# A decoder block by split float32 products: the rotary exchange moved to ScalarE, and five more steps by seven products

## The chip, the cores and the metric

The kernel runs on one core of one Trainium2 chip, in one launch. The metric is the device time of the launch in microseconds (us), the median of several runs. TensorE is called PE, VectorE DVE, ScalarE ACT and SyncE SP, as the profile does.

## The reference

One layer of a decoder block for 256 positions of width 2048, all in float32. Shortened to what is computed:

```python
a = rmsnorm(h, norm_mix_pre)
q_a, k_a, v_a, q_r, f_r, i_r, g_r, gate_a, gate_r = split_columns(a @ w_in)     # 2048 x 17408
qh, kh = rotary(heads(q_a), S), rotary(heads(k_a), S)    # rot = [-t[64:], t[:64]]; t * cos + rot * sin
attn = dilated_window_attention(...)      # 3 groups of 8 heads, mixed by their denominators
r_out = hgrn2_chunked(silu(q_r), log f, 1 - f, i_r)      # gated recurrence, normed, times silu(g_r)
y = sigmoid(gate_a) * (attn @ w_attn_branch) + sigmoid(gate_r) * (r_out @ w_hgrn_branch)
h = h + rmsnorm(y @ w_mix_out, norm_mix_post)
gt, up = split(rmsnorm(h, norm_ffn_pre) @ w_ffn_gate_up)     # 2048 x 11264
ff = (silu(gt) * up) @ w_ffn_down                        # 5632 x 2048
h = h + rmsnorm(ff, norm_ffn_post)
```

## The kernel before

Every weight matrix is streamed from HBM once. To keep float32 accuracy with the fast `fp32r` matmul, each weight and each activation is split into a high part (ACT copies it with rounding) and a low part (DVE subtracts: raw minus high), and each product is three matmuls: high x high, high x low, low x high. `mm` at L138 records nearly all of PE's matmuls, so most rows of PE carry that line.

The work is a list `items` that the loop at L1600 walks. An item is either a *chunk* (128 x 1024 weights, 16 matmuls in its common form; the stages of f, q, the rotary q and k, the branches) or a *step* of a *wide block* (two groups of 512 columns by 256 rows). The items' order is written out by hand, and so is what runs beside an item. In iteration `i`, `prepare(i)` splits item `i + 2` (AHEAD = 2), fetches sums for item `i + 4` and issues the load of raw weights as far as three raw buffers allow; then `multiply(i)` issues PE's work; then generators that wait in queues are advanced by one `yield` each: `evacs` (emptying PSUM), `lanes` (attention, recurrence, norms) and, in chunk items, `back` (weight sums). All engines run their instructions in that order, so an instruction that waits holds up what is behind it on its engine.

A wide step (m, 0) is plain: 2 x 2 x 2 products of 128 x 128 x 512, three matmuls each, 24 matmuls. A step "by seven" computes the same with seven products of sums of the operands, Strassen's way: 21 matmuls. It needs sums of the weights and sums of the activations (`seven_sums`, `pair_sums`, kept in `h7` for the FFN). In (m, 1) DVE forms the weights' sums (`sum`, L434, L440, L441), ACT and DVE split them into `hi` and `lo` (L439, L442, L447) and split three quarters of the raw weights into `dh` and `dl` (L445, L449). In (m, 2) the sums were formed long before, by `weight_sums`, and stored to DRAM as `presum`; `fetch_sums` brings them back as `s`, and only the splits are left (L426 to L430). `dh` and `dl` share four slots (tag "d"). Products go to eight PSUM banks, four called `acc` and four `aux`; in a block whose `flip` is false, the four plain sums take aux banks and the products p1, p5, p6 and p7 take acc banks. Within a step by seven PE first does the products of sums and then those of raw weights; in the last one of a block, and in the down blocks, the other way round.

After a block's last step by seven, `gather` (L506) joins p1, p5, p6 and p7; `evac_ffn` (L1376) adds them at the block's end; `turn_act` (L1339), after step 1 of the next block, transposes the finished block's output on PE into two PSUM banks (acc where `flip` is false), from which ACT copies it (L1349).

The FFN's gate and up weights are 11 blocks of 8 steps, numbered 0 to 10 by `j` at L1574; block 0 is plain, and GATE_UP3 and GATE_UP4 give the order of steps in the others. `w_ffn_down` follows as two blocks of 22 steps; there `prep_act` splits the activations and makes their sums for each step by seven.

`weight_sums` (L294) is one generator for all steps (m, 2). For each it loads 1 MB into the one buffer `pre`, lets four items pass, forms the sums with four DVE instructions in two items, and stores `presum` from ACT's queue; it moves by one `yield` per chunk item and is put off while `hold` is set in `recurrence`.

`evac_rope` (L873) applies the rotary step to a q or k block of two heads, transposed (head dimension in partitions): two DVE products of 64 partitions write the exchanged halves times sin to `w`, one more multiplies by cos, one adds.

Of the kernel before, what the change touches and what calls it, by code (L numbers as in the profile page):

```python
# [21 lines left out]
S = 256  # L22
# [19 lines left out]
    [(2, 0), (3, 0), (0, 1), (4, 0), (1, 1), (5, 0), (6, 0), (7, 0)],  # L42
]
GATE_UP3 = [(3, 0), (4, 0), (0, 2), (5, 0), (1, 1), (6, 0), (2, 2), (7, 0)]
GATE_UP4 = [(4, 0), (5, 0), (0, 2), (6, 0), (1, 1), (2, 2), (3, 1), (7, 0)]
PLACE = (0, 2, 1, 3)
DOWN = [[(m, m in by7) for m in range(KF // 2)] for by7 in (range(4, 20, 3), range(3, 19, 3))]

N_F, N_RAW, N_SPLIT, AHEAD, WARM, BRIDGE = 15, 3, 3, 2, 8, 6

# [50 lines left out]
def tile_hybrid_block(ctx: ExitStack, tc: tile.TileContext, t, out):  # L101
# [192 lines left out]
    def weight_sums(jobs):  # L294

        for n in jobs:
            x = fp[0].tile([P, 2048], F32, tag="pre", bufs=1, name=nm("pre"))
            b, i = steps[n][:2]
            m = b.order[i][0]
            for g in range(2):  # L300
                nc.sync.dma_start(
                    x[:, g * 1024 : (g + 1) * 1024].rearrange("p (k c) -> p k c", k=2),
                    b.w[2 * m * P : (2 * m + 2) * P, b.cols[g] : b.cols[g] + 512]
                    .rearrange("(k p) c -> p k c", p=P),
                )
            for _ in range(4):
                yield
            r = [x[:, q * 512 : (q + 1) * 512] for q in range(4)]
            nc.vector.tensor_sub(r[2], r[2], r[0])
            nc.vector.tensor_sub(r[0], r[1], r[0])  # L310
            yield
            nc.vector.tensor_add(r[1], r[1], r[2])
            nc.vector.tensor_sub(r[3], r[3], r[1])
            yield
            pre[n] = dram.tile([P, 2048], F32, name=nm("presum"))
            nc.scalar.dma_start(pre[n], x)
            yield
# [327 lines left out]
        return row[:, None, :].to_broadcast([P, n, S])  # L645

    evacs, turns, lanes, queue = deque(), deque(), [deque(), deque()], deque()
    back, hold = deque(), [False]
    ready = set()

    def advance(q):
# [43 lines left out]
    def opening():  # L695
        ss, s2 = small("ss"), small("s2")
        yield from sumsq(ss, xt)
        nc.sync.dma_start(gainr, t["hgrn_norm_gain"].to_broadcast([P, HW]))
        nc.sync.dma_start(cs, t["rope"])
        add_parts(s2[:, :2], ss)  # L700
        rsqrt_mean(r1c, s2[:, :2], D)
        ready.add("r1c")
        nc.scalar.preload_act_table_set("silu_and_others")
        yield from row_broadcast(rowb, r1c)
        ready.add("rowb")
        yield
        for _ in range(24):
            yield
        for i, (j, c) in enumerate(((0, -QSCALE), (1, -QSCALE), (0, 1.0), (1, 1.0))):
            nc.vector.scalar_tensor_tensor(  # L710
                out=tabs[:, i, :], in0=cs[:, j, :], scalar=c, in1=rowb, op0=OP.mult, op1=OP.mult
            )
            yield
        nc.sync.dma_start(amask, t["amask"])
        nc.sync.dma_start(lmask, t["lmask"])
# [157 lines left out]
    def evac_rope(key, tab, then=None):  # L873

        cos = tabs[:, tab, :]
        sin = tabs[:, tab + 1, :]

        def ev(i, src):
            if i == 0:
                qkT[key] = fslot("qk").rearrange("p (h t) -> p h t", h=4)  # L880
            yield
            w = ptile("w").rearrange("p (h t) -> p h t", h=2)
            for o, n in ((0, 64), (64, 0)):
                nc.vector.tensor_mul(
                    w[o : o + 64], src[n : n + 64],
                    sin[n : n + 64, None, :].to_broadcast([64, 2, S]),
                )
            yield
            u = src
            nc.vector.tensor_mul(u, src, by_rows(cos, 2))  # L890
            nc.vector.tensor_add(
                qkT[key][:, 2 * i : 2 * i + 2, :].rearrange("p h (two j) -> p h two j", two=2),
                u.rearrange("p h (j two) -> p h two j", two=2),
                w.rearrange("p h (j two) -> p h two j", two=2),
            )
            if i == 1 and then:
                then()
        return ev
# [339 lines left out]
    def mix_to_ffn(i):  # L1238
# [60 lines left out]
        ffn(2, 1)  # L1299
        residual_of(5, (0, 1), False)  # L1300

    def more_h(c):
        if c + 1 < KD // 2:
            transpose_in(h_t, colg[:, 16:32], hT[0], c + 1)
# [3 lines left out]
            residual_of(7, (0, 1), False)  # L1308
            lanes[0].append(second_norm())
        if c == 4:  # L1310
            lanes[1].append(pair_sums(hT[0], h7, lambda: rslot("so"), range(4)))

    def second_norm():
        ss, s2 = small("ss"), small("s2")
# [86 lines left out]
    def prep_act(m, by7):  # L1401
# [6 lines left out]
        x.high(0, f)  # L1408
        yield
        x.low(0, f)  # L1410
        if by7:
            dst = rslot("so").rearrange("p (z n t) -> p z n t", z=2, n=4)
            high, low = seven_sums(f, dst)
            high()
            a7[m] = sums_of(dst)
            yield
            low()
# [154 lines left out]
    add_wide_block(w, (0, FF), PLAIN, lambda k: hT[0](k), None, evac_first, True, mid=more_h)  # L1572
    spare = wides[-1], 0
    for j in range(1, 11):  # L1574
        add_wide_block(w, (512 * j, FF + 512 * j), GATE_UP4 if j > 1 else GATE_UP3, lambda k: hT[0](k),
                       lambda m: h7[m], evac_ffn, j % 2 == 0,
                       pre=begin_wides if j == 1 else None, turn=1)
    for j in range(2):
# [19 lines left out]
    split(1)  # L1598
    load_upto(AHEAD + N_RAW - 1)
    for i in range(len(items)):  # L1600
        kind, n, _ = items[i]
        b, c = kind[n][:2]
        wide = kind is steps
        if wide:
# [96 lines left out]
```

## Time and profile before

| | us |
|---|---|
| median of 3 runs (lowest, highest) | 1697.41 (1697.04, 1697.93) |
| the profiled execution, its time | 1698.13 |
| the profiled execution, its span | 1696.3 |

| engine | busy us | share of the span |
|---|---|---|
| PE, matmuls | 1685.2 | 99% |
| PE, weight loads | 1416.7 | 84% |
| DVE | 1436.2 | 85% |
| ACT | 914.7 | 54% |

The profile is of one execution. Times in its rows are us from the span's start, means are ns. A timeline row gives start, length, engine, line, operation, what is written from what, shape, count, and in brackets how long the engine had been idle and what ended that. A busy PE may still be slowed, since matmuls overlap; the distance between their starts shows their pace. The granted clock is 0.998 over the span.

### The profile page before, as it was taken

The numbers are of one execution on the slowest core, as the hardware profiler recorded it, in microseconds if no ns is written. First come the engines' busy times: TensorE is split into PE (matmuls) and PEld (weight loads), VectorE is DVE, ScalarE is ACT, GpSimd is POOL, SyncE is SP. The second block draws the span as 40 slices with busy tenths as digits, with TensorE's granted clock in tenths as the row PEclk, the third lists the DMA queues.
The fourth block names the chain that finished last, engine by engine and source line by source line (L and its number), as shares of the span: only waits on it lengthen the run. The fifth ranks groups of instructions, "written<-read, shape, count | busy, mean of one in ns | idle before, by whom it ended". The sixth has DMA issues, their size and how long they took to land.

```text
span 1696.3 us, 21711 instructions
## 1 busy us (share of the span) xinstructions
PE 1685.2 (99%) x8260; PEld 1416.7 (84%) x8260; DVE 1436.2 (85%) x1662; ACT 914.7 (54%) x1034; POOL 3.9 (0%) x13
## 2 busy tenths in 40 slices
PE   9999999999999999999999999999999999999997
PEld 7888888888888888888888888888888888888886
DVE  6999888867998988885668888888888888898997
ACT  6655555544444434445445547555555555565663
POOL 0000000000000000000000000000000000000000
PEclk9999999999999999999999999999999999999999
DMA  8667666768677767787858646777777777777773
GB/s 285 205 224 243 230 233 228 234 222 309 225 254 252 256 223 243 253 310 275 295 172 275 210 162 227 269 250 252 254 255 253 249 248 272 257 266 256 248 244 130
DMA packets 228904, 413.48 MB, mean 244 GB/s; under 512 B 12816, under 2 KB 79552, under 8 KB 226240
## 3 DMA queue, kind: packets, MB, share of 16 engines
q1 hardware_dynamic: 218544, 373.93, 65.4%
q10 hardware_dynamic: 10192, 38.15, 6.0%
q8 instruction: 64, 1.05, 0.3%
q14 instruction: 40, 0.33, 0.1%
q0 software_dynamic: 64, 0.02, 0.0%
HBM read 376.92 MB, written 35.13 MB: 243 GB/s over the span
## 4 chain that ended last, share of the span: by engine, by line
PE 98%; DVE 1%; ACT 0%; issue 0%; DVEq 0%; ACTq 0%
PE acc L138 62%; PE aux L138 34%; PE aux L930 0%; DVE wl L420 0%; PE aux L610 0%; PE aux L1348 0%; DVE fz L1475 0%; PE acc L1348 0%; ACT w L418 0%; ACT junk L1429 0%; PE aux L597 0%; DVE e L1425 0%; PE aux L1110 0%; DVE yT L578 0%; PE aux L1220 0%
## 5 line engine op out<-in xcount | busy, mean ns | idle before, releaser
L138 PE MATMUL acc<-xT,w 128*128 128x256 f32 (+1 forms) x2048 | 366.8, 338 | 0.0
L420 DVE TENSOR_TENSOR wl<-raw,w 128x2048 fp32r<-128x2048 f32 (+1 forms) x141 | 306.6, 2182 | 68.8 <-ACT w L418 67.1
L138 PEld LDWEIGHTS acc<-xT,w 128*128 128x128 f32 x2048 | 311.9, 188 | 44.7 <-DVE w L365 0.3
L418 ACT ACTIVATE w<-raw 128x2048 fp32r<-128x2048 f32 (+1 forms) x141 | 256.3, 1827 | 109.3 <-PE acc L138 35.1
L364 ACT ACTIVATE w<-raw 128x1024 fp32r<-128x1024 f32 x176 | 185.7, 1058 | 220.5 <-PE acc L138 169.6
L365 DVE TENSOR_TENSOR w<-raw,w 128x1024 fp32r<-128x1024 f32 x176 | 214.8, 1221 | 95.9 <-ACT w L364 95.2
L138 PE MATMUL acc<-w,xT 128*128 128x512 f32 x578 | 169.1, 392 | 0.0
L439 ACT ACTIVATE w<-sum 128x1024 fp32r<-128x1024 f32 x56 | 59.5, 1063 | 177.8 <-DVE sum L434 170.6
L138 PE MATMUL acc<-w,hT 128*128 128x512 f32 x472 | 152.7, 391 | 0.4 <-DVE hT L1232 0.4
L447 DVE TENSOR_TENSOR wl<-sum,w 128x1024 fp32r<-128x1024 f32 x112 | 134.8, 1221 | 13.2 <-ACT w L439 13.2
L138 PEld LDWEIGHTS acc<-w,xT 128*128 128x128 f32 x578 | 108.1, 188 | 22.2
L138 PE MATMUL aux<-w,hT 128*128 128x512 f32 x374 | 120.0, 389 | 0.0
L449 DVE TENSOR_TENSOR dl<-raw,dh 128x1536 fp32r<-128x1536 f32 x56 | 98.3, 1756 | 14.3 <-ACT dh L445 12.2
L138 PE MATMUL aux<-w,xT 128*128 128x512 f32 x344 | 109.8, 389 | 0.0
L138 PEld LDWEIGHTS acc<-w,hT 128*128 128x128 f32 x472 | 88.5, 188 | 19.0 <-DVE hT L1232 0.8
L138 PE MATMUL acc<-wl,hT 128*128 128x512 f32 x236 | 91.9, 389 | 0.0
L445 ACT ACTIVATE dh<-raw 128x1536 fp32r<-128x1536 f32 x56 | 82.7, 1476 | 8.0 <-PE aux L138 4.4
L138 PE MATMUL acc<-w,a 128*128 128x512 f32 x268 | 83.7, 389 | 0.0
L138 PE MATMUL aux<-w,a 128*128 128x512 f32 x268 | 83.7, 389 | 0.0
L138 PEld LDWEIGHTS aux<-w,hT 128*128 128x128 f32 x374 | 70.2, 188 | 14.6
L138 PE MATMUL acc<-w,so 128*128 128x512 f32 x234 | 78.8, 391 | 0.0
L138 PEld LDWEIGHTS aux<-w,xT 128*128 128x128 f32 x344 | 64.6, 188 | 13.4
(298 smaller groups left out, 2964.3 us busy)
## 6 DMA issues: line engine op xcount, KB each, us to landing
raw<-in_w_in SPq DMA_DIRECT2D x270, 512.0 KB, 4.8
raw<-in_w_ffn_gate_up SPq DMA_DIRECT2D x156, 512.0 KB, 4.8
raw<-in_w_ffn_down SPq DMA_DIRECT2D x88, 512.0 KB, 5.4
pre<-in_w_ffn_gate_up SPq DMA_DIRECT2D x40, 512.0 KB, 6.5
presum<-pre ACTq DMA_DIRECT2D x20, 1024.0 KB, 4.7
s<-presum SPq DMA_DIRECT2D x40, 512.0 KB, 7.0
raw<-in_w_mix_out SPq DMA_DIRECT2D x32, 512.0 KB, 4.9
act<-acts SPq DMA_DIRECT2D x22, 512.0 KB, 6.5
```

Of the source, the lines that this page charges most:

```text
L138: nc.tensor.matmul(ps, lhsT, rhs, start=start, stop=stop, skip_group_check=True)
L364: nc.scalar.activation(wh, raw, AF.Copy)
L365: nc.vector.tensor_sub(wl, raw, wh.bitcast(F32))
L418: nc.scalar.activation(hi[:, c], raw[:, c], AF.Copy)
L420: nc.vector.tensor_sub(lo[:, c], raw[:, c], hi[:, c].bitcast(F32))
L439: nc.scalar.activation(hi[:, :1024], s[:, :1024], AF.Copy)
L445: nc.scalar.activation(dhi, d, AF.Copy)
L447: nc.vector.tensor_sub(lo[:, c], s[:, c], hi[:, c].bitcast(F32))
L449: nc.vector.tensor_sub(dlo, d, dhi.bitcast(F32))
```

## The change

Four things change.

1. The rotary step: ACT copies the two halves crosswise into `w` (two instructions of 64 partitions), and one DVE product over all 128 partitions multiplies `w` by sin. The signs of the sin rows in `tabs` are adapted.
2. Blocks 3, 5, 7 and 9 of the FFN follow GATE_UP5: five steps by seven instead of four, (4, 2) being new, and these five stand one behind the other. That makes 24 sets of weight sums instead of 20. `h7` holds five sets, four of them in slots of the pool that `zg` used.
3. `weight_sums` goes faster once the first rotary block is there: a load begins on an odd item, and three items pass instead of four.
4. The second down block has steps (2), (4), (7), (10), (13), (16) and (18) by seven instead of (3), (6), (9), (12), (15) and (18); sums of activations that the first down block made for the same m are used again.

```diff
+GATE_UP5 = [(5, 0), (6, 0), (0, 2), (1, 1), (2, 2), (4, 2), (3, 1), (7, 0)]
 GATE_UP4 = [(4, 0), (5, 0), (0, 2), (6, 0), (1, 1), (2, 2), (3, 1), (7, 0)]
-DOWN = [[... for by7 in (range(4, 20, 3), range(3, 19, 3))]
+DOWN = [[... for by7 in (range(4, 20, 3), (2, 4, 7, 10, 13, 16, 18))]
...
     def weight_sums(jobs):
         for n in jobs:
+            quick = ("q", 0, 0) in qkT
+            while quick and count[0] % 2 == 0:
+                yield
...
-            for _ in range(4):
+            for _ in range(3 if quick else 4):
                 yield
...
-        for i, (j, c) in enumerate(((0, -QSCALE), (1, -QSCALE), (0, 1.0), (1, 1.0))):
+        for i, (j, c) in enumerate(((0, -QSCALE), (1, QSCALE), (0, 1.0), (1, -1.0))):
...
             for o, n in ((0, 64), (64, 0)):
-                nc.vector.tensor_mul(
-                    w[o : o + 64], src[n : n + 64],
-                    sin[n : n + 64, None, :].to_broadcast([64, 2, S]),
-                )
+                nc.scalar.activation(w[o : o + 64], src[n : n + 64], AF.Copy)
             yield
             u = src
             nc.vector.tensor_mul(u, src, by_rows(cos, 2))
+            nc.vector.tensor_mul(w, w, by_rows(sin, 2))
...
+    def h7_slot():
+        return p3("so", F32R, 1024, 4) if len(h7) < 4 else rslot("so")
...
-            lanes[1].append(pair_sums(hT[0], h7, lambda: rslot("so"), range(4)))
+            lanes[1].append(pair_sums(hT[0], h7, h7_slot, range(5)))
...
-        if by7:
+        if by7 and m not in a7:
             dst = rslot("so").rearrange("p (z n t) -> p z n t", z=2, n=4)
...
+        order = GATE_UP3 if j == 1 else GATE_UP5 if j in (3, 5, 7, 9) else GATE_UP4
+        add_wide_block(w, (512 * j, FF + 512 * j), order, lambda k: hT[0](k),
```

What this moves, in block 3 of the FFN (blocks 5, 7 and 9 are alike). First ACT's order before: `w` is a high part, `dh` that of raw weights, `s` the fetched sums, `sum` those formed on DVE, `act` the copy of the transposed previous block (L1349).

```order
L426 ACTIVATE w_9301<-s_9227 128x1024
L426 ACTIVATE w_9301<-s_9228 128x1024
L429 ACTIVATE dh_9307<-raw_9199 128x1536
L418 ACTIVATE w_9344<-raw_9231 128x2048
L1349 ACTIVATE act_9379<-acc_9380 128x512
L1349 ACTIVATE act_9379<-acc_9386 128x512
L1353 DMA acts_9392<-act_9379 128x1024
L439 ACTIVATE w_9394<-sum_9396 128x1024
L442 ACTIVATE w_9394<-sum_9396 128x1024
L445 ACTIVATE dh_9402<-raw_9268 128x1536
```

And ACT's order now, at the same place (the same lines have other numbers: L426 is L430, L439 L443, L442 L446, L445 L449, L1349 L1354).

```order
L430 ACTIVATE w_9371<-s_9297 128x1024
L430 ACTIVATE w_9371<-s_9298 128x1024
L433 ACTIVATE dh_9377<-raw_9269 128x1536
L443 ACTIVATE w_9418<-sum_9420 128x1024
L446 ACTIVATE w_9418<-sum_9420 128x1024
L449 ACTIVATE dh_9426<-raw_9301 128x1536
L1354 ACTIVATE act_9463<-acc_9464 128x512
L1354 ACTIVATE act_9463<-acc_9470 128x512
L1358 DMA acts_9476<-act_9463 128x1024
L430 ACTIVATE w_9478<-s_9381 128x1024
```

Before, one copy for the plain step (6, 0) stood ahead of the two copies of `act`; now the three copies for step (1, 1) do, two of which read sums that DVE forms. Second, DVE's order before, from the split of (2, 2) to that of the second plain step behind (3, 1):

```order
L427 TENSOR_TENSOR wl_9437<-s_9348,w_9436 128x1024
L427 TENSOR_TENSOR wl_9437<-s_9349,w_9436 128x1024
L430 TENSOR_TENSOR dl_9443<-raw_9311,dh_9442 128x1536
L434 TENSOR_TENSOR sum_9475<-raw_9352 128x1024
L440 TENSOR_TENSOR sum_9475<-raw_9352,sum_9475 128x512
L441 TENSOR_TENSOR sum_9475<-raw_9352,sum_9475 128x512
L447 TENSOR_TENSOR wl_9474<-sum_9475,w_9473 128x1024 x2
L449 TENSOR_TENSOR dl_9482<-raw_9352,dh_9481 128x1536
L420 TENSOR_TENSOR wl_9512<-raw_9408,w_9511 128x2048
L420 TENSOR_TENSOR wl_9540<-raw_9446,w_9539 128x2048
```

And DVE's order now, from the split of (2, 2) to the first plain step:

```order
L431 TENSOR_TENSOR wl_9479<-s_9381,w_9478 128x1024
L431 TENSOR_TENSOR wl_9479<-s_9382,w_9478 128x1024
L434 TENSOR_TENSOR dl_9485<-raw_9338,dh_9484 128x1536
L431 TENSOR_TENSOR wl_9517<-s_9432,w_9516 128x1024
L431 TENSOR_TENSOR wl_9517<-s_9433,w_9516 128x1024
L434 TENSOR_TENSOR dl_9523<-raw_9385,dh_9522 128x1536
L438 TENSOR_TENSOR sum_9552<-raw_9436 128x1024
L444 TENSOR_TENSOR sum_9552<-raw_9436,sum_9552 128x512
L445 TENSOR_TENSOR sum_9552<-raw_9436,sum_9552 128x512
L451 TENSOR_TENSOR wl_9551<-sum_9552,w_9550 128x1024 x2
L453 TENSOR_TENSOR dl_9559<-raw_9436,dh_9558 128x1536
L424 TENSOR_TENSOR wl_9589<-raw_9488,w_9588 128x2048
```

Between the splits of (2, 2) and (3, 1) the three instructions of (4, 2) have come in, whose last, `dl_9523`, needs `dh_9522` in the slots of step (1, 1).

More of the change, by code (lines that the diff above doesn't have):

```diff
@@ L44 @@
 GATE_UP3 = [(3, 0), (4, 0), (0, 2), (5, 0), (1, 1), (6, 0), (2, 2), (7, 0)]
+GATE_UP5 = [(5, 0), (6, 0), (0, 2), (1, 1), (2, 2), (4, 2), (3, 1), (7, 0)]
 GATE_UP4 = [(4, 0), (5, 0), (0, 2), (6, 0), (1, 1), (2, 2), (3, 1), (7, 0)]
 PLACE = (0, 2, 1, 3)
-DOWN = [[(m, m in by7) for m in range(KF // 2)] for by7 in (range(4, 20, 3), range(3, 19, 3))]
+DOWN = [[(m, m in by7) for m in range(KF // 2)] for by7 in (range(4, 20, 3), (2, 4, 7, 10, 13, 16, 18))]
 N_F, N_RAW, N_SPLIT, AHEAD, WARM, BRIDGE = 15, 3, 3, 2, 8, 6
@@ L647, in tile_hybrid_block @@
     evacs, turns, lanes, queue = deque(), deque(), [deque(), deque()], deque()
-    back, hold = deque(), [False]
+    back, hold, count = deque(), [False], [0]
     ready = set()
@@ L1574, in tile_hybrid_block @@
     for j in range(1, 11):
-        add_wide_block(w, (512 * j, FF + 512 * j), GATE_UP4 if j > 1 else GATE_UP3, lambda k: hT[0](k),
+        order = GATE_UP3 if j == 1 else GATE_UP5 if j in (3, 5, 7, 9) else GATE_UP4
+        add_wide_block(w, (512 * j, FF + 512 * j), order, lambda k: hT[0](k),
                        lambda m: h7[m], evac_ffn, j % 2 == 0,
@@ L1600, in tile_hybrid_block @@
     for i in range(len(items)):
-        kind, n, _ = items[i]
+        count[0], (kind, n, _) = i, items[i]
         b, c = kind[n][:2]
```

## The prediction

> **What bounds the kernel now.** I read the page's busy times first, then the list of what PE waited for, then the chain of waits, then the engines' timelines in one gate/up block.
>
> ```profile
> PE 1685.2 (99%) x8260; PEld 1416.7 (84%) x8260; DVE 1436.2 (85%) x1662; ACT 914.7 (54%) x1034; POOL 3.9 (0%) x13
> ...
> PE acc L138 <- DVE hT L1232: 0.4, 1, 0.4
> PE acc L138 <- DVE gate L1147: 0.2, 1, 0.2
> ```
>
> The last two rows are all that PE waited for between the kernel's start and its end: 0.6 us. So time leaves this kernel only as PE work, and comes back only where PE is made to wait. How fast PE streams is in the chain of waits (start, length, what, count):
>
> ```profile
> 472.62 8.43 PE acc L138 x48
> ...
> 582.16 8.66 PE acc L138 x48
> ...
> 1115.27 6.12 PE acc L138 x27
> 1121.39 10.88 PE aux L138 x48
> ```
>
> In the FFN 10.88 / 48 = 6.12 / 27 = 0.2267 us per matmul of 512 columns: a plain step (24 matmuls) takes 5.44 us and a step by seven (21) 4.76 us. A chunk of 16 matmuls in the rotary stage takes 8.43 / 3 = 2.81 us. The windows (PE, PEld, DVE, ACT, POOL busy, clock, DMA share, GB/s) show the rotary stage and the FFN:
>
> ```profile
> 440.00:520.00 80.00, 80.00 (x512) 71.15 (x512) 72.59 (x100) 34.14 (x50) 0.00 (x0) 1.00 0.73 249
> 1200.00:1300.00 100.00, 100.00 (x456) 83.05 (x455) 87.30 (x79) 56.69 (x50) 0.00 (x0) 1.00 0.74 253
> ```
>
> PE never pauses in either, and VectorE has 9% and 13% left: a small margin for a change that alters what VectorE does and when.
>
> **Term 1, the PE work removed.** Five steps go from plain to by seven (one in each of blocks 3, 5, 7, 9, and in the second down block seven by seven instead of six): 5 x 3 = 15 matmuls x 0.2267 = **-3.40 us**. The count is exact; nothing else on PE changes. The Trainium skill (Perfetto Trace Analysis, Identifying the Most-Contended Engine) says matmul busy time misleads and weight-load busy share should be read; that is 84% here, and by it I would credit only 0.84 x 3.40 = 2.9 us, making the sum 0.5 us higher. The pitch above decides against it: each matmul starts 0.2267 us after the last, whatever the load's share.
>
> **Term 2, a bank wait in the four blocks.** A block with five by seven splits (1,1) one step sooner: right behind (0,2), where the plain (6,0) stood. So ScalarE has the three copies for (1,1) ahead of the first copy of the transposed block (L1349), and PE's third product of (0,2), p7, needs the PSUM bank that this copy empties: of four acc banks two hold the transposes, p6 and p5 take the others. From block 5 before (VectorE, ScalarE, PE; start, length):
>
> ```profile
> 1212.36 2.28 DVE L420 TENSOR_TENSOR wl<-raw,w 128x2048 fp32r<-128x2048 f32 x1
> 1214.56 1.22 DVE L434 TENSOR_TENSOR sum<-raw 128x1024 f32<-128x1024 f32 x1
> 1215.81 0.69 DVE L440 TENSOR_TENSOR sum<-raw,sum 128x512 f32<-128x512 f32 x1
> 1216.54 0.69 DVE L441 TENSOR_TENSOR sum<-raw,sum 128x512 f32<-128x512 f32 x1
> ...
> 1216.14 1.09 ACT L1349 ACTIVATE act<-acc 128x512 f32<-128x512 f32 x2 [3.91 <-PE acc L1348]
> ...
> 1218.59 1.05 ACT L442 ACTIVATE w<-sum 128x1024 fp32r<-128x1024 f32 x1
> 1219.55 1.47 ACT L445 ACTIVATE dh<-raw 128x1536 fp32r<-128x1536 f32 x1
> ...
> 1215.50 1.03 PE L1348 MATMUL acc<-ident,e 128*128 128x128 f32 x8
> 1216.29 0.48 PE L138 MATMUL acc<-w,so 128*128 128x512 f32 x1
> ...
> 1217.53 0.61 PE L138 MATMUL acc<-w,so 128*128 128x512 f32 x2
> ```
>
> Now L434 stands where L420 began, 1212.36. L440 follows 1.25 later, L441 0.73 after that, ending at 1215.03. L442 (second half of (1,1)'s high part) starts then, L445 0.96 later, and the first L1349 1.38 after that (1.47 less the 0.09 by which ScalarE's operations overlap): 1217.4 instead of 1216.14. One copy is half of 1.09 and a little, 0.6: the bank is free at 1218.0. p7 is the seventh matmul of the step, 1217.53 + 0.23 = 1217.75. In the kernel before that cover is a full 1.0 us; now it is gone by 0.25 to 0.3. PE pays a little more than the wait, as its one long wait shows:
>
> ```profile
> 1004.87 0.40 PE L138 MATMUL acc<-wl,hT 128*128 128x512 f32 x1
> 1005.68 0.73 PE L138 MATMUL acc<-w,hT 128*128 128x512 f32 x2 [0.41 <-DVE hT L1232]
> 1006.25 0.39 PE L138 MATMUL acc<-wl,hT 128*128 128x512 f32 x1
> ```
>
> There two matmuls took 0.57 instead of 0.45: 0.11 more behind a wait. So 0.4 us a block, x 4 = **+1.6 us**. Ends: 0 (the copy 0.3 earlier) and +2.8 (0.3 later).
>
> **Term 3, the last step by seven of the four blocks.** (3,1) is the last by seven of its block and begins with its raw products, so PE needs its dh and dl at once. dh and dl come from four slots, two steps' worth. Before, (6,0) stood between and only (3,1) had to wait for an earlier step ((1,1)) to give its slots back; now five by seven stand in a row, (4,2) must wait for (1,1) to end, and (3,1)'s VectorE work is queued behind (4,2)'s dl. In block 5 before:
>
> ```profile
> 1231.32 1.49 ACT L445 ACTIVATE dh<-raw 128x1536 fp32r<-128x1536 f32 x1 [0.89 <-PE acc L138]
> ...
> 1226.66 1.22 DVE L434 TENSOR_TENSOR sum<-raw 128x1024 f32<-128x1024 f32 x1
> ...
> 1232.85 1.76 DVE L449 TENSOR_TENSOR dl<-raw,dh 128x1536 fp32r<-128x1536 f32 x1 [1.16 <-ACT dh L445]
> 1234.65 4.49 DVE L420 TENSOR_TENSOR wl<-raw,w 128x2048 fp32r<-128x2048 f32 x2
> ...
> 1229.37 1.06 ACT L442 ACTIVATE w<-sum 128x1024 fp32r<-128x1024 f32 x1 [0.33 <-DVE sum L441]
> ...
> 1236.34 0.39 PE L138 MATMUL aux<-dl,hT 128*128 128x512 f32 x1
> ```
>
> The first row is the moment T at which (1,1) ends on PE. From it dl is done and VectorE free at 1234.65, T + 3.33; PE needs dl one step and one matmul after T, at 1236.34, and has it 1.7 us early. In the changed kernel those 3.33 us are (4,2)'s. Then (3,1) starts: L434 to L442 is 2.71 (1226.66 to 1229.37), L442 to dh 0.96, dh to dl 1.53, dl 1.76: T + 3.33 + 6.96 = T + 10.29. PE needs it two steps and one matmul after T: 2 x 4.76 + 0.23 = T + 9.75. A wait of 0.54, and 0.11 behind it: 0.65 x 4 = **+2.6 us**. The interval is counted from (1,1)'s own end, so term 2 does not shorten it. Ends: +1.2 and +4.0 (the chain 0.35 shorter or longer).
>
> **Term 4, the second down block.** It has (2) and (4) by seven where (3) was the first. VectorE and PE at its start:
>
> ```profile
> 1571.27 0.39 PE L138 MATMUL aux<-w,a 128*128 128x512 f32 x1
> ...
> 1572.58 0.68 DVE L578 TENSOR_TENSOR a<-act,a 128x512 fp32r<-128x512 f32 x1
> ...
> 1576.30 1.22 DVE L434 TENSOR_TENSOR sum<-raw 128x1024 f32<-128x1024 f32 x1
> ...
> 1584.96 0.74 DVE L1434 SCALAR_TENSOR_TENSOR fz<-e,r2c,fpost 128x512 f32<-128x512 f32 x1
> 1585.62 0.68 DVE L578 TENSOR_TENSOR a<-act,a 128x512 fp32r<-128x512 f32 x1
> ...
> 1588.43 0.74 DVE L1434 SCALAR_TENSOR_TENSOR fz<-e,r2c,fpost 128x512 f32<-128x512 f32 x1
> ```
>
> A split by seven takes 8.66 (1576.30 to 1584.96), a gain 0.66, a plain split 2.81. A step whose sums exist from the first block saves about 1.5 and takes 7.2. From 1572.58: 8.66 + 0.66 + 2.81 + 0.66 + 7.2 = 1592.57. PE comes to (4) at 1571.27 + 3 x 5.44 + 4.76 = 1592.35 and needs dl at 1592.58: a tie. **+0.2 us**; ends 0 and +0.8. The four sums no longer made (6 us of VectorE) are off PE's path later in the block and are counted at nothing.
>
> **Term 5, the rotary stage.** Per block of the stage one VectorE product falls away and ScalarE gets two copies of 64 rows (the nearest ScalarE row has 128 rows of 512; on VectorE 64 rows cost 0.686 by L884 and 128 rows 0.69 by L440 above, so I take it whole):
>
> ```profile
> L884 DVE TENSOR_TENSOR w<-sum,tabs 64x512 f32<-64x512 f32 x48 | 33.0, 686 | 1.1
> ...
> L528 ACT ACTIVATE so<-s 128x512 fp32r<-128x512 f32 x21 | 13.2, 631 | 13.4 <-DVE s L526 13.4
> ```
>
> VectorE: -24 x 0.69 = -16.5 us, plus four more weight sums, 4 x 4 x 0.69 = +11 us. ScalarE: +48 x 0.63 = +30 us, which its 57% idle time takes. Since PE did not pause, nothing of VectorE's 5.5 us comes off the end. But from ("q", 0, 0) on a weight sum has its four VectorE instructions three items after its loads instead of four, 2.81 us sooner:
>
> ```profile
> DMA to landing us min/median/max: 3.9/6.2/8.4
> ...
> 613.67 1.02 SPq L301 DMA_DIRECT2D pre<-in_w_ffn_gate_up  x2
> ...
> 621.94 0.69 DVE L309 TENSOR_TENSOR pre<-pre 128x512 f32<-128x512 f32 x1 [0.40 <-issue]
> ```
>
> That sum before already found VectorE waiting 0.40, 7.8 us after its second load was issued (613.67 plus half of 1.02). With 3 x 2.81 = 8.4 us less what SP is late, VectorE will stand at some of the 20 quick sums for 1 to 3 us, with the chunk splits, the rotary product and the recurrence's products queued behind it. Splits are two chunks ahead (5.6 us), so most of that is covered; a recurrence product that PE takes in the next item is not. I take three waits of 0.3: **+1.0 us**. Ends: -0.2 (the piece of 8.66 above against 8.43, if it goes) and +4 (ten waits of 0.4).
> The Trainium skill (Perfetto Trace Analysis, Optimizing Scalar/DVE Operations) holds that work moved to ScalarE from a saturated VectorE can pay; by it this term would be -0.2 and the sum +0.8, inside rival A.
>
> At nothing: the other signs in the table (the same four instructions), the fifth pair of h sums (made two blocks before block 3 uses it), the other slots for h sums.
>
> **The sum:** -3.40 + 1.6 + 2.6 + 0.2 + 1.0 = **+2.0 us**. The profiled execution took 1698.13 (span 1696.3, 1.8 around it), so 1700.1 there; it lies 0.7 above the median of 1697.41, so the median becomes **1699.4**.
>
> **Rivals.**
> A, the forecast: the removed matmuls are paid back by new PE waits, -1 to +3.4. Chance 0.70.
> B, all covers hold: ScalarE reaches the transposed copy 0.3 us sooner and (3,1)'s dl is 0.6 sooner. Then -3.4 to -3.6, 1693.8 to 1694.0. For it: PE pauses nowhere in the FFN now, and 0.3 and 0.6 are small against chains of ten instructions. Against it: both chains are read off neighbouring rows. It decides at these 0.3 and 0.6. Chance 0.08.
> C, slower: the presum loads. If VectorE stands 2 us at ten of the quick sums and the recurrence or the splits run dry, PE waits ten times 0.4 and the sum is +5, 1702.4. It decides at a landing of over about 7 us after the load's issue; the row gives a median of 6.2 and a maximum of 8.4. Chance 0.16.
> D, slower: the weights' transfers in the five steps by seven.
>
> ```profile
> 1225.00:1227.00 2.00, 2.00 (x10) 1.68 (x9) 2.00 (x3) 0.00 (x0) 0.00 (x0) 1.00 1.04 393
> ```
>
> Three steps with fetched sums (1.84 MB) and two without (1.05 MB) are 7.6 MB in 5 x 4.76 us, 319 GB/s, under the 393 that the queues reach. If slots come free too late to use that, 1 us more a block: +6, 1703.4. Chance 0.06.
>
> **The numbers.** A measurement can tell about 0.2% (3.4 us) from no change: faster is below 1694.0, slower above 1700.8. A lies within but for a tenth of its chance at the top; B sits on the lower border, half of it beyond, and a little of A's; C lies two thirds above. Faster 0.05, same 0.73, slower 0.22. The range 1696.2 to 1702.6 leaves out B and the upper part of C and D.
>
> **What would show it.** Waits of PE in blocks 3, 5, 7 and 9 alone: one on ScalarE's L1354 copy at the third product of (0,2), about 0.3; one on dl of (3,1), about 0.5. No PE wait there makes it B; waits for raw or s transfers make it D. VectorE waiting for pre's transfers at L313, and PE waits between 450 and 870 us, size term 5. I am wrong if the waits at the two places are missing or twice as long.

## The result and the profile after

| | us |
|---|---|
| median of 6 runs before (lowest, highest) | 1697.77 (1697.04, 1698.13) |
| median of 6 runs after (lowest, highest) | 1703.26 (1701.82, 1705.87) |
| after / before, 95% interval | 1.0035 (1.0024 to 1.0045) |
| the profiled execution after, its time and span | 1702.24, 1700.5 |

The changed kernel is 5.5 us slower. The forecast was 1699.4, with a range up to 1702.6; the result lies above it. First the page's busy times and then all that PE waited for between the start and the end (us in total, times, longest):

```profile
PE 1684.5 (99%) x8245; PEld 1412.4 (83%) x8245; DVE 1435.5 (84%) x1653; ACT 951.0 (56%) x1089; POOL 3.9 (0%) x13
...
PE acc L139 <- DVE w L369: 2.0, 3, 1.1
...
PE aux L139 <- DVE q L1042: 1.1, 1, 1.1
PE aux L139 <- DVE dl L453: 1.0, 4, 0.3
PE acc L139 <- DVE hT L1234: 0.4, 1, 0.4
PE acc L139 <- DVE gate L1149: 0.2, 1, 0.2
```

The 15 matmuls are gone (8260 before). The last two rows are the two waits of the kernel before; the other three are new. The shares of busy time show nothing of this: PE stands at 99% in both pages.

**In the FFN** the two forecast waits are there. Block 5, PE (start, length, count, and in brackets the idle time):

```profile
1220.76 1.01 PE L139 MATMUL acc<-w,so 128*128 128x512 f32 x2
1221.62 0.40 PE L139 MATMUL acc<-wl,so 128*128 128x512 f32 x1
...
1239.09 0.39 PE L139 MATMUL aux<-dh,hT 128*128 128x512 f32 x1
1239.73 0.50 PE L139 MATMUL aux<-dl,hT 128*128 128x512 f32 x1 [0.26 <-DVE dl L453]
1240.07 0.39 PE L139 MATMUL aux<-dh,hT 128*128 128x512 f32 x1
```

The two matmuls from 1220.76 take 0.86 instead of 2 x 0.2267: 0.41 for the bank. PE's row carries no bracket, because it was the load of the matmul's weights (PEld) that waited; among the waits of PEld stand those of the four blocks:

```profile
PEld acc L139 <- ACT act L1354: 2.2, 4, 0.6
```

From 1239.09 two matmuls take 0.98: 0.53 for dl. ACT's row tells the bank's story:

```profile
1219.27 1.47 ACT L449 ACTIVATE dh<-raw 128x1536 fp32r<-128x1536 f32 x1
1220.65 1.06 ACT L1354 ACTIVATE act<-acc 128x512 f32<-128x512 f32 x2
```

The first copy begins 1.38 behind L449's start, and its bank is free half of 1.06 later, 1221.2; the seventh matmul of the step, due at 1221.0, is the one that came late. 0.94 a block, 3.7 us in the four.

**In the rotary stage** DVE now stands for the loads of the weight sums. Waits between 350 and 900 us, before and then after, and the summary of `pre`:

```profile
DVE pre L309 <- DMA pre<-in_w_ffn_gate_up: 1.5, 2, 0.8
DVE pre L309 <- issue: 0.4, 1, 0.4
```

```profile
DVE pre L313 <- DMA pre<-in_w_ffn_gate_up: 16.2, 11, 4.2
DVE pre L313 <- issue: 4.9, 2, 3.3
...
DMA to landing us min/median/max: 3.8/6.4/10.8
```

13 of 24 sets wait, 21.1 us together; 11 of them are among the 20 quick ones. Before SP can issue a load it must often wait until the last set has been stored from the same buffer (before, then after):

```profile
SPq L301 <- DMA presum<-pre: 11.5, 7, 3.2
```

```profile
SPq L305 <- DMA presum<-pre: 28.5, 13, 6.6
```

What one of DVE's waits does, DVE's timeline and then PE's:

```profile
583.24 0.69 DVE L313 TENSOR_TENSOR pre<-pre 128x512 f32<-128x512 f32 x1 [4.21 <-DMA pre<-in_w_ffn_gate_up]
583.96 0.69 DVE L314 TENSOR_TENSOR pre<-pre 128x512 f32<-128x512 f32 x1
584.57 1.22 DVE L369 TENSOR_TENSOR w<-raw,w 128x1024 fp32r<-128x1024 f32 x1
585.71 0.68 DVE L316 TENSOR_TENSOR pre<-pre 128x512 f32<-128x512 f32 x1
586.43 0.69 DVE L317 TENSOR_TENSOR pre<-pre 128x512 f32<-128x512 f32 x1
587.04 1.22 DVE L369 TENSOR_TENSOR w<-raw,w 128x1024 fp32r<-128x1024 f32 x1
```

```profile
585.85 5.61 PE L139 MATMUL acc<-xT,w 128*128 128x256 f32 x31 [1.07 <-DVE w L369]
592.58 1.66 PE L139 MATMUL aux<-q,kk 128*128 128x64 f32 x13 [1.12 <-DVE q L1042]
```

DVE idles 4.21 us, then has two of the sums to do before the split that PE already needs, and stays late long enough to make a recurrence product late as well. Counted by the distances between starts PE has four such waits (at 556, 586, 592 and 773 us), 4.0 us in all, against 0.3 in the kernel before. Three are for a chunk split, one is for the recurrence product. So the profiled execution adds up: 1698.13 - 3.4 + 3.7 + 4.0 - 0.3 = 1702.1, measured 1702.24.

### The profile page after: what moved, and what is told of

It is laid out like the page before. It is cut to its first block, busy times and chain, and to the rows that moved or that the text cites. A ratio compares the mean times of both kernels' runs of the same rounds, so it can differ in the third digit from the quotient of the medians.

```text
span 1700.5 us, 21764 instructions
## 1 busy us (share of the span) xinstructions
PE 1684.5 (99%) x8245; PEld 1412.4 (83%) x8245; DVE 1435.5 (84%) x1653; ACT 951.0 (56%) x1089; POOL 3.9 (0%) x13
## 4 chain that ended last, share of the span: by engine, by line
PE 86%; DVE 6%; issue 3%; ACT 3%; DMA 3%; DVEq 0%; SPq 0%; ACTq 0%
PE acc L139 55%; PE aux L139 29%; DMA raw<-in_w_in 1%; DVE w L369 1%; DMA presum<-pre 1%; DMA pre<-in_w_ffn_gate_up 1%; ACT w L422 1%; DVE sum L438 1%; ACT dh L449 0%; DVE e L1384 0%; DVE dl L453 0%; PE aux L932 0%; DVE wl L424 0%; ACT dh L433 0%; DVE sum L445 0%
## 5 line engine op out<-in xcount | busy, mean ns | idle before, releaser
L424 DVE TENSOR_TENSOR wl<-raw,w 128x2048 fp32r<-128x2048 f32 (+1 forms) x136 | 295.4, 2180 | 65.8 <-ACT w L422 64.0
L422 ACT ACTIVATE w<-raw 128x2048 fp32r<-128x2048 f32 (+1 forms) x136 | 246.8, 1823 | 99.0 <-PE acc L139 31.8
L443 ACT ACTIVATE w<-sum 128x1024 fp32r<-128x1024 f32 x57 | 60.6, 1063 | 197.5 <-DVE sum L438 192.0
L453 DVE TENSOR_TENSOR dl<-raw,dh 128x1536 fp32r<-128x1536 f32 x57 | 100.1, 1757 | 10.9 <-ACT dh L449 8.9
L139 PE MATMUL aux<-w,hT 128*128 128x512 f32 x318 | 102.8, 389 | 0.0
L139 PE MATMUL acc<-w,so 128*128 128x512 f32 x264 | 89.9, 392 | 0.5
L449 ACT ACTIVATE dh<-raw 128x1536 fp32r<-128x1536 f32 x57 | 84.0, 1474 | 4.4 <-PE aux L139 4.4
L139 PE MATMUL aux<-w,a 128*128 128x512 f32 x254 | 79.4, 389 | 0.0
L139 PE MATMUL acc<-wl,xT 128*128 128x512 f32 x193 | 75.1, 389 | 0.0
```

Source lines behind the costliest of these rows:

```text
L139: nc.tensor.matmul(ps, lhsT, rhs, start=start, stop=stop, skip_group_check=True)
L422: nc.scalar.activation(hi[:, c], raw[:, c], AF.Copy)
L424: nc.vector.tensor_sub(lo[:, c], raw[:, c], hi[:, c].bitcast(F32))
L443: nc.scalar.activation(hi[:, :1024], s[:, :1024], AF.Copy)
L449: nc.scalar.activation(dhi, d, AF.Copy)
L453: nc.vector.tensor_sub(dlo, d, dhi.bitcast(F32))
```

## The experiments

The kernel before took 1697.6 to 1698.3 beside them (medians). A table first; the last column is DVE's waits in front of the first sum of a set, in us. Rows with "..." and the last four build on the other order.

| run | us (lowest, highest) | ratio to before, 95% | DVE waits for pre |
|---|---|---|---|
| rotary step alone | 1698.35 (1697.05, 1699.02) | 1.0001 (0.9993 to 1.0010) | 3.9 |
| quick pace alone | 1705.46 (1705.05, 1707.37) | 1.0047 (1.0033 to 1.0061) | 15.7 |
| other order of the five | 1700.80 (1698.95, 1701.89) | 1.0017 (1.0008 to 1.0025) | 19.1 |
| ... sums on GpSimd | 1710.45 (1708.09, 1711.67) | 1.0073 (1.0060 to 1.0085) | none |
| ... sums in one item, an item later | 1699.66 (1697.56, 1701.63) | 1.0009 (1.0000 to 1.0018) | 5.8 |
| ... transfers from GpSimd's queue | 1706.18 (1705.90, 1707.17) | 1.0049 (1.0036 to 1.0063) | 33.1 |
| ... the same, sums five items behind | 1701.08 (1699.85, 1702.19) | 1.0020 (1.0011 to 1.0029) | 29.8 |
| ... by halves | 1719.91 (1715.71, 1723.55) | 1.0126 (1.0111 to 1.0140) | 57.7 |
| ... no loads | 1694.92 (1694.16, 1695.93) | 0.9981 (0.9972 to 0.9989) | 0.4 |
| ... no sums | 1694.88 (1694.08, 1695.66) | 0.9980 (0.9970 to 0.9989) | none |
| 22 sets, quick outside the rotary stage | 1700.93 (1698.48, 1703.59) | 1.0017 (1.0009 to 1.0026) | 12.9 |
| 21 sets, old pace | 1696.38 (1695.96, 1696.94) | 0.9993 (0.9984 to 1.0001) | 2.7 |
| 22 sets, quick from 720 us | 1696.19 (1695.42, 1696.76) | 0.9991 (0.9982 to 1.0000) | 2.5 |
| 23 sets, quick from 600 us | 1696.79 (1695.83, 1699.89) | 0.9997 (0.9989 to 1.0006) | 14.6 |

### The parts by themselves

**Rotary step alone**: the kernel before with the `evac_rope` and `tabs` lines of the diff.

> The kernel before with the rotary exchange on ScalarE alone. Theory P (pace: the time lost in the rotary stage comes from VectorE standing at the weight sums for pre's transfers): nothing changes at the end, 1697.2 to 1698.4, and VectorE waits for pre no longer than before (1.9 us in all). Theory S (ScalarE's 48 copies stand ahead of the chunk splits and make them late): 1701 to 1704, with PE waits between 450 and 870 us.

1698.35 against 1697.79: no change. PE's waits are those of the kernel before.

**Quick pace alone**: the kernel before with the `weight_sums` lines of the diff (20 sets).

> The kernel before with the quicker weight sums alone (load on an odd item, three items instead of four; 20 sets, all orders as before). Theory P: 1700 to 1704, VectorE waits for pre 12 us or more in ten or more sums, and PE waits 2 to 5 us between 450 and 870 us. Theory S: within 1 us of before, since ScalarE has no copies here.

+7.7 us, more than the whole change costs and more than the 1704 that theory P allowed. Its waits:

```profile
PE acc L138 <- DVE w L368: 4.0, 5, 1.8
...
DVE pre L312 <- DMA pre<-in_w_ffn_gate_up: 13.6, 10, 3.8
```

So the pace alone makes the loss in this stage; the rotary step on ACT is not its cause, and may soften it (its own price was not told apart from chance).

**The order of the five**: the changed kernel with

```diff
-GATE_UP5 = [(5, 0), (6, 0), (0, 2), (1, 1), (2, 2), (4, 2), (3, 1), (7, 0)]
+GATE_UP5 = [(5, 0), (6, 0), (0, 2), (2, 2), (1, 1), (3, 1), (4, 2), (7, 0)]
```

> The changed kernel with another order of steps in blocks 3, 5, 7 and 9: (5,0) (6,0) (0,2) (2,2) (1,1) (3,1) (4,2) (7,0), still five by seven. Theory O (the two waits of each block come from the order: the copies of (1,1) ahead of the transposed copy, and a last step by seven whose sums VectorE still has to form): both waits go from all four blocks, 4 x (0.40 + 0.52) = 3.7 us less than the changed kernel, 1699.6 (1698.3 to 1701). Theory L (VectorE's load or the transfers of five steps by seven are too much, in whatever order): the waits come back elsewhere in the blocks, 1702.5 to 1704.

The ratio falls from 1.0035 to 1.0017, 3 us, and PE waits for nothing in the gate and up blocks any more: the FFN waits were the order's. What is left:

```profile
PE acc L139 <- DVE w L369: 2.5, 3, 0.9
...
PE aux L139 <- DVE q L1042: 1.1, 1, 1.1
```

All runs behind this one keep this order.

### What of the quick pace costs

**Sums on GpSimd**: `nc.vector` becomes `nc.gpsimd` in the four additions of `weight_sums`.

> As e4_order, and the four additions of each weight sum on GpSimd instead of VectorE; loads, pace and ScalarE's stores stay. Theory P: VectorE waits for pre nowhere, PE waits in the rotary stage nowhere or under 1 us in all; with the FFN's waits gone too the 15 matmuls show in full: 1697.8 - 3.4 = 1694.4 (1693.8 to 1695.5). Theory S: the rotary stage stays as slow, 1699 to 1700. If GpSimd slows VectorE where both work, means of VectorE's rows between 450 and 870 us rise, and 1696 or more.

Missed by 16 us. DVE waits for no load, but two other things happen. First, some of its own instructions became slow. Groups (us in total, mean ns) between 350 and 900 us, here and then in the run with the order alone:

```profile
L316 POOL TENSOR_TENSOR pre<-pre 128x512 f32<-128x512 f32 x24 | 43.5, 1811 | 1.9
...
L242 DVE TENSOR_TENSOR sum<-acc,sum 128x256 f32<-128x256 f32 x64 | 23.9, 413 | 0.0
...
L891 DVE TENSOR_TENSOR sum<-sum,tabs 128x512 f32<-128x512 f32 x24 | 21.8, 910 | 0.0
```

```profile
L242 DVE TENSOR_TENSOR sum<-acc,sum 128x256 f32<-128x256 f32 x64 | 23.9, 415 | 0.0
...
L891 DVE TENSOR_TENSOR sum<-sum,tabs 128x512 f32<-128x512 f32 x24 | 16.4, 683 | 0.0
```

The product of two operands in SBUF went from 683 to 910 ns, the one that reads PSUM stayed (see the hardware below). Second, GpSimd now stands in front of the load, and ACT's store of the sums, with ACT's copies behind it, waits for GpSimd's last addition:

```profile
ACT w L368 <- POOL pre L317: 44.6, 8, 9.3
```

With the order alone ACT waited 22.8 us in 7 such places. The chain into PE's wait at 417 us runs load, four additions, ACT's store, ACT's copy, DVE's split. So the wait for the load had only moved to another engine; what each of the two things costs was not told apart.

**Sums an item later, in one item**: the wait is four items again; the `yield` between the two pairs of sums falls away.

> The changed kernel with the better order of the blocks by five, and the quick pace altered: the sums wait four items behind their load again instead of three, and all four DVE instructions stand in one item instead of two, so that a set still takes as many items as in the changed kernel. The order alone gave 1700.8 us. Theory T (the sums stand one item too soon: DVE waits for the 1 MB of weights, and its late splits hold PE up): DVE's waits for pre fall from some 20 us to under 6, PE's waits for w of L369 from 2.5 us to under 1, and the time is 1695.5 to 1698. Theory Q (the pace itself: with a set every six items, SP waits for the store of the sums before it may refill the one buffer, and the raw weights behind it come late): SP's waits for presum stay near 28 us, and the time stays at 1699.5 to 1701.5. A third way (four DVE instructions of 0.69 us in one item hold the evictions up): DVE's waits fall but the time stays above 1699.

DVE's waits fall from 19.1 to 5.8 us, SP's for `presum` from 27.7 to 15.1, and the time by 1 us only: above theory T's 1695.5 to 1698, and theory Q's condition (SP's waits stay) is not met either. It is the third way: four sums in a row hold up as well. PE waits 1.5 us at 591, behind a load wait of 3.0 and four sums, and 1.0 us at 698, behind four sums with no load wait. The profiled execution took 1697.82, below the median, so these waits are not all that the median holds.

**Transfers from GpSimd's queue**: both `dma_start` of `weight_sums` go to `nc.gpsimd`.

> The changed kernel with the better order of the blocks by five, and with both transfers of the weight sums, the load of pre and the store of presum, issued from GpSimd's queue instead of SP's and ACT's. The sums stay three items behind their load, on DVE. The order alone gave 1700.8 us. Theory Q (SP, which waits for the store of the sums, and ACT, whose store waits for DVE's last sum, hold up what is behind them): SP's waits for presum (28 us) are gone, ACT's waits for pre (22.8 us) too, and the time falls to 1694.5 to 1697. Theory T (DVE waits for the 1 MB itself, which takes 7 to 8 us from its issue whichever queue issues it): DVE still waits over 12 us for pre, and the time stays at 1699 to 1701.5.

SP and ACT no longer wait for any of it, and the kernel is 5 us slower, not faster: theory Q's forecast fails, and theory T's upper end of 1701.5 is passed too. Since DVE's waits rose as well, this run alone can't say that SP's and ACT's waits were free. The trace of the changed kernel says more: in the rotary stage none of ACT's copies waits for raw weights, which theory Q needs. The chain of waits that ends in PE's longest pause (start, length):

```profile
812.23 10.49 DMA presum<-pre
...
823.81 8.01 DMA pre<-in_w_ffn_gate_up
...
833.28 1.22 DVE w L369
```

The one buffer must be stored (10.49) before it is loaded (8.01), and DVE stood 7.2 us in front of it; the table's 33.1 us are the sum of all such waits. PE's pause of 4.7 us has a price behind it too: from 834.3 to 840 us its granted clock is 0.54, which is another 0.46 x 5.7 = 2.6 us.

**The same with the sums five items behind the load**, the next load right behind the store, a set every six items.

> The changed kernel with the better order of the blocks by five; the transfers of the weight sums issued from GpSimd's queue; the next load stands right behind the store in that queue, and the sums stand five items behind it, two DVE instructions in each of two items; a set every six items, on even and odd items alike. Both theories T (sums too soon) and Q (waits of SP and ACT) expect the cost of the sums to be gone: DVE waits under 3 us for pre, PE's waits in the stage of the rotary step within 0.6 us of those of the kernel before (L369 1.1 us), and so a time of before less what PE saves: 1697.8 - 3.4 + 0 to 0.8 = 1694.4 to 1695.2. If it stays above 1698, the cost is neither, but the four DVE instructions or the 1 MB each way themselves (theory S).

1701.08: five items did not cover it either. DVE still waits 29.8 us, not under 3, so theory S is not tested by this run. (The 1.1 us that the expectation gives for the kernel before is not in its profile, which shows 0.3 us there, by the distances.) The chain into its first long wait holds a store of 5.4 us, a load of 7.6 and the sums, one behind the other, where six items of 2.81 us are 16.9.

**By halves**: 256 columns at a time in two buffers of half the size; load of the next half, three items, four sums, an item, store.

> The changed kernel with the better order of the blocks by five, all 24 sets, but the weight sums done by halves: 256 columns of each group at a time in two buffers of half the size (the same room). A half's load is issued three items ahead of its four DVE instructions (256 elements instead of 512), into the buffer whose store was issued two items before; a set still takes six items. The order alone gave 1700.8 us, the sums in one item 1699.7. If it is the single buffer that costs (theory Q: SP waits 28 us for stores, ACT 23 us for the last sum; theory T: DVE waits 14 to 20 us for loads issued late), SP's waits for presum fall under 6 us, DVE's for pre under 6, and the time comes to 1694.5 to 1697. If it is the sums and bytes themselves at this pace (theory S: 24 sets of DVE work and 48 MB of transfers within the stage), the time stays above 1699.

A clear miss, 1719.91: the halves are loaded three items ahead each, so DVE waits 22 times instead of 11, 57.7 us, and ACT, whose store stands behind the sums, 70.8 us. It does not test theory S either.

**No loads, and no sums**: two kernels with the same pace. The first loads `pre` for the first set only; the second leaves out the four additions and keeps every transfer.

> The changed kernel with the better order and its quick pace, but the loads of pre are left out behind the first (the sums are formed again and again from what lies in the buffer, and stored as before, so the weights of the steps fed by them are not right). DVE's work, the stores and the pace stay. Theories T and Q (the load that SP issues late and DVE waits for): DVE's waits for pre and SP's for presum are gone, and the time falls from 1700.8 to 1694.4 to 1696. Theory S (DVE's 4 x 0.69 us a set at this pace, or the stores): 1699 to 1701.

> The changed kernel with the better order and its quick pace, but the four DVE instructions of each set are left out: the raw weights are loaded and stored again unchanged (so the weights of the steps fed by them are not right). Loads, stores, SP's waits for the store before each load and the pace stay; DVE waits for no load. Theory T (DVE's wait for the load delays the splits that PE needs) and theory S (DVE's own work): 1694.4 to 1696, PE's waits for w of L369 under 1.2 us. Theory Q (SP's waits delay the raw weights): SP still waits 20 us or more for presum, and the time is 1697.5 to 1701.

1694.92 and 1694.88, the expected 1698.25 - 3.4 = 1694.9 to the tenth. All that PE waits for in the second, but for the warming matmuls at the start:

```profile
PE acc L139 <- DVE hT L1230: 0.4, 1, 0.4
PE acc L139 <- DVE gate L1145: 0.2, 1, 0.2
```

Either half of the work is free; only the two together cost. Theory S (the work itself) falls with the first, and the transfers' cost with the second. What both runs took away is DVE's wait in front of the loaded data, but also waits that hang on it: SP's for `presum` (27.7 us with the order alone) were gone in the first and 10.9 in the second, not the 20 expected, and ACT's for the last sum (22.8) were 8.9 and none. So the two runs alone do not single out DVE's wait; the traces do. ACT waited 20.0 us for last sums in the kernel before, at no cost to PE, and 22.8 in the changed one; DVE's wait for the load went from 1.9 to 21.1, and a load wait of DVE stands in front of each of PE's four waits.

### Which sets may be quick

**21 sets at the old pace**: block 9 alone by five, `weight_sums` as before.

> The changed kernel with the better order, but one block by five (block 9) instead of four, so that there are 21 sets of weight sums, and these at the pace of the kernel before (four items behind the load, any item). The rotary step on ACT and the second down block are as in the changed kernel. PE saves 6 matmuls, 6 x 0.2267 = 1.36 us. Theories T and Q (the cost is the quick pace): 1697.8 - 1.4 = 1696.4, 1695.5 to 1697.5, with DVE's waits for pre under 5 us in all. Theory S (each set costs by itself, whatever its pace): 1697.8 - 1.4 + 1/4 of 4 = 1697.4; little apart, so that the waits decide: PE's waits for w of L369 stay near 1.1 us by T and Q.

1696.38, as expected. PE's share of the chain of waits is back at

```profile
PE 98%; DVE 1%; ACT 0%; issue 0%; DVEq 0%; ACTq 0%
```

(86% in the changed kernel).

**22 sets, quick outside the rotary stage**: blocks 7 and 9; six items a set before the first rotary block and from item 195 on.

> The changed kernel with the better order, two blocks by five (7 and 9), so 22 sets of weight sums. Pace: as in the kernel before within the stage of the rotary step; before the first rotary block and from item 195 on (some 780 us) a set takes six items, with the sums four items behind the load and in one item. PE saves 9 matmuls, 2.04 us. If the cost lies in the quick pace within the rotary stage alone: 1697.7 - 2.0 = 1695.7, 1694.8 to 1696.6, and PE has no wait over 0.5 us between 540 and 880 us that the kernel before hasn't. If the quick pace costs wherever it runs (theory S): 1696.5 to 1698.

Missed: 1700.93, above the range of theory S too. PE waits 1.8 us at 390 and at 426 us, in the first chunks, where I had thought there was room, and 1.2 us at 597, within the rotary stage and behind a load wait of 2.9 at the old pace. The chain into the first:

```profile
376.62 1.24 DVE w L368
...
377.87 0.37 SPq L270
...
378.89 0.45 SPq L303
...
379.38 7.48 DMA pre<-in_w_ffn_gate_up
...
386.94 0.70 DVE pre L311
...
389.73 1.23 DVE w L368
...
391.00 1.09 PE acc L139 x5
```

This is a loop that I had not seen. SP issues the load of `pre` (L303) behind that of raw weights (L270), which waits for DVE's split to free a raw slot. So the load starts when DVE has done the split, not so many items earlier as the code says; 7.48 later DVE has its data, does the sums, and only then the next split. A late DVE makes its own load late. In the changed kernel it is mostly the store that holds the load back: SP issues the load within 0.1 us of the store's landing at 536.6 and 758.4 us, ahead of DVE's waits at 543 and 766. The longest wait there, at 583 us, has another cause: its load was issued at 571 and 573 us and took over 10 us to land.

**22 sets, quick late only** (from item 180), and **23 sets, quick from item 145**: `quick = count[0] >= 180` (145), the wait of four items always, sums in one item where quick.

> The changed kernel with the better order, two blocks by five (7 and 9), so 22 sets. The pace of the kernel before up to item 180; from there on (some 720 us) a set takes six items, its sums four items behind the load and in one item. The run with 22 sets that was quick before the first rotary block too had its waits at 390, 426, 432 and 597 us, and none behind 620. If the quick pace costs only where DVE's sums wait for their load while PE is close behind DVE (the first chunks and the rotary blocks up to 600 us), the time is 1697.8 - 2.0 = 1695.8, 1694.9 to 1696.7, with no wait of PE between 350 and 880 us that the kernel before hasn't. If the four sums in one item, or a set every six items, cost by themselves: waits behind 720 us, and 1697 to 1700.

> As the run with 22 sets and the quick pace late, but three blocks by five (5, 7 and 9), 23 sets, and the quick pace from item 145 on (some 600 us), through most of the rotary stage. PE saves 12 matmuls, 2.72 us. If the quick pace costs only up to 600 us: 1697.8 - 2.7 = 1695.1, 1694.2 to 1696.2. If it costs wherever DVE is over three quarters busy (DVE 76% between 620 and 780 us, 65% behind): a wait of PE for w of L369 between 620 and 720 us, as the sums in one item with 24 sets had at 698 us (1.0 us), and 1696 to 1698.5.

1696.19, as expected: PE has no new wait at all in the first. In the second it has one:

```profile
PE acc L139 <- DVE w L368: 1.4, 1, 1.4
```

at 748 us, not where I had expected it, and with it 1696.79. So a set is not dear by itself. As I read it, it costs where DVE's wait for the load, with the sums behind it, is longer than DVE's lead over PE at that place: at 748 us a wait of 2.4 and four sums of 0.7 were too much. The lead itself was not measured place by place. Behind 780 us, where DVE is busy 58 to 60 us of 90, quick sets were free in these two runs, a load wait of 3.2 us included.

The version with 22 sets that is quick late has the lowest median of the complete kernels: its highest time, 1696.76, is under the lowest of before, 1696.97, though 1.5 us are less than the 0.2% named in the prediction. From the 21 sets at the old pace (1696.38) it can't be told apart.

## Why the prediction was wrong

**What failed is term 5, the cover of the splits.** The step was "Splits are two chunks ahead (5.6 us), so most of that is covered ... I take three waits of 0.3: +1.0 us", with an end of +4. The profiled execution has four waits of 0.6 to 1.4, 4.0 us less 0.3 that were there before, and three of the four are for the splits that the step held covered; with the FFN's waits gone the median still lies 1700.8 - (1697.8 - 3.4) = 6.4 above what the removed matmuls alone would leave. The start of the mechanism was right (DVE "will stand at some of the 20 quick sums for 1 to 3 us"): 11 stood, eight of them 1.5 to 4.2. Wrong were two things. I set the lead of 5.6 us against the wait alone, but the sums stand between the wait and the split: 4.21 + 2 x 0.7 at 583 us already use it up. And I took the load's issue as fixed by the item. In the changed kernel it follows the store of the set before (SP waits for that 28.5 us, 11.5 before; a store took up to 10.5), and in the run with 22 sets it followed DVE's split through SP. In the run with the order alone, four waits, 4.8 us counted in the same way, and a stretch at half clock (1.7, told below), less the 0.3, make 6.2 in its profiled execution; what the changed kernel's median holds beyond its profiled 3.7 was not traced.

**Rival C was this case** and had 0.16. Its threshold was a landing of over 7 us (the summary has up to 10.8); its price for this stage, ten waits of 0.4, stands against 3.7 in the profiled execution and 1703.26 - (1697.77 - 3.4 + 3.7) = 5.2 by the medians. It deserved the larger chance: before the change the row with 0.40 us already showed a sum without cover, and the change took 2.8 us more from it, 20 times over.

**Term 1** held: -3.40 forecast, -3.3 and -3.4 measured in the two runs without the stage's cost. The credit of 2.9 by the weight-load share, which the prediction weighed from the Trainium skill (Perfetto Trace Analysis, Identifying the Most-Contended Engine), is inside those runs' intervals (the wider, 0.9970 to 0.9989, is 1.9 to 5.1 us), so they don't exclude it; the trace's pitch of 0.2267 does.

**Term 2** held: 0.40 a block forecast, 0.41 measured, on ACT's copy at the seventh matmul. **Term 3**: 0.65 forecast, 0.53 measured; dl came 0.12 sooner than the chain of neighbouring rows gave. Both forecast in place and nearly in size: +4.2 against 3.7. The run with the other order took both away; of its 3 us less, 3.7 were expected. **Term 4**: 0.2 forecast; at 1597 us there is 0.1. **Rival B** (all covers hold) and **D** (transfers) did not occur: PE waits for no s or raw transfer in the blocks.

**The rotary step itself** was counted at -16.5 us of DVE and +30 us of ACT with nothing at the end; alone it gave +0.6 within an interval of -1.2 to +1.7. So it cost and brought nothing that can be told, and the gain for which the Trainium skill (Perfetto Trace Analysis, Optimizing Scalar/DVE Operations) was cited there was not seen.

With 3.7 measured for terms 2 and 3, the forecast would have missed by term 5 alone.

## What to carry to other kernels

Price a wait on an in-order engine together with the work that stands between it and what the next engine needs, and compare that sum with the lead. Then ask what issues the awaited transfer: if that queue itself waits for the engine, the lead written in the code (so many items) is not the lead in time. Faster feeding is worth trying only where the engine has room, and one that saves 0.68 us a set must not cost more than that in one wait.

## What the hardware showed besides

**Half pace behind short waits.** In the run with the order alone PE's granted clock fell to half after waits of 1.1 and 1.3 us at 586 and 592.5 us. Windows of that run, then of the kernel before (length, busy times, then the granted clock, the DMA share and GB/s):

```profile
594.00:600.50 6.50, 6.26 (x33) 5.65 (x34) 6.50 (x11) 1.48 (x3) 0.00 (x0) 0.74 0.66 210
```

```profile
594.00:600.50 6.50, 6.50 (x40) 5.73 (x39) 6.41 (x10) 2.12 (x2) 0.00 (x0) 1.00 0.89 298
```

At half pace for 3.4 of 6.5 us (0.26 x 6.5 / 0.5) PE loses 1.7 us more. The changed kernel had waits of the same length 6.7 us apart and kept its clock, so the price of a wait varies from run to run. That may be part of the spread of the changed kernel's times (4 us, against 1 before), which was not shown. In the run with the sums in one item the times and the mean clocks do go together: 0.998 to 0.999 in the five executions below 1698.2 us, 0.996 in the two above 1701.5. The Trainium skill (TensorE: Matmul & The Clock Gate, Why this matters for your kernels) warns of idle gaps over some 3 us. Here the clock fell with no gap so long; that the two short ones did it is likely, not shown. In the run with the transfers on GpSimd's queue it fell within a pause of 4.7 us, as the page has it. The free-running window of 3.4 us that the Trainium skill gives (same page, What's actually happening) agrees with the length of the slow stretch, and would explain the chance in it.

**GpSimd slows DVE.** The addition at L316, 128 x 512, takes GpSimd 1811 ns and DVE 684, and in the run where GpSimd adds, some of DVE's instructions take far longer (min/median/max):

```profile
L891 DVE TENSOR_TENSOR sum<-sum,tabs x24: 675/684/1783, 463.5 to 774.6; 128x512 f32<-128x512 f32 x24
```

The median is untouched and the longest is 2.6 times as long. Of these 24, 19 took 675 to 685 ns and five 1761 to 1783: each was either free or held. The Trainium skill (SBUF — State Buffer, SBUF: two separate sides) says of the port pair that the two share that it is locked for a whole instruction; these rows agree, also in that the sum out of PSUM (L242) is not slowed.
